# Two decoder layers on one core: 64-byte pads that shift the weight buffers and the streamed operands in SBUF

## The chip, the cores and the metric

The kernel runs on one core of one Trainium2 chip. The metric is the device time of one execution in microseconds, the median of several runs. Before the change it is 2217.02 us.

## What is computed

Two decoder layers over 256 tokens of width 2048, all in float32. The first layer mixes by sliding-window attention (32 query heads, 8 key and value heads, learned sinks), the second by a gated linear recurrence (RG-LRU). Each is followed by a gated MLP with a short causal convolution. Cut to what sets the work:

```python
D_MODEL, SEQ, DEPTH = 2048, 256, 2
QKV_DIM, D_FF = 3072, 6144

# layer 0: attention
qkv = h @ w_qkv                       # [256, 2048] @ [2048, 3072]
...
x = x + out.reshape(B, T, 2048) @ w_o
# layer 1: recurrence
xb, yb = jnp.split(h @ w_in, 2, axis=-1)   # [2048, 4096]
...
x = x + (hs * gate) @ w_out
# behind each of the two
u = causal_dwconv(h @ w_up, conv_w, conv_b)     # [2048, 12288]
g, v = jnp.split(u, 2, axis=-1)
x = x + (jax.nn.gelu(g, approximate=True) * v) @ w_down   # [6144, 2048]
```

Here `h` is the RMS-normed `x` each time.

## The kernel before

Activations stay in SBUF, transposed: features on the 128 partitions, the 256 tokens along the free axis. The weights are read once, in 373 chunks of 1 MiB (128 x 2048 float32). A chunk goes by DMA into a buffer `raw`; ScalarE casts it to `hi` (line 109), VectorE makes `lo = raw - hi` (line 117), and TensorE multiplies with both. Each of the three has three buffers in a pool of its own.

A product of two float32 numbers is taken as hi\*hi + hi\*lo + lo\*hi. A block of 128 x 128 of the weights is the stationary operand, loaded by an instruction of its own (LDWEIGHTS), and the activations are streamed past it. `mm_hi` (line 183) loads a block of `hi` and streams 512 columns, the activation's two parts side by side; `mm_lo` (line 189) loads a block of `lo` and streams 256 columns, the first part. A chunk has 16 blocks, so it costs a group of 16 matmuls of 512 columns and then a group of 16 of 256. In the MLP's down projection the chunk is taken in two halves of 8 and 8.

The products are named by their PSUM tiles: `pk`, `pq` (keys, queries), `po` (attention's output), `pu`, `pd` (MLP up and down, twice each), `px`, `py` (the recurrence's two input branches), `pr` (its output); for `pv` (values) the activation is stationary and the weight streams. The streamed operand is `h` in `pk`, `pq`, `pu`, `px` and `py`; it is `ao` in `po`, `g` in `pd` and `z` in `pr`. Between the chunks of `px` the small gate products `g<-xc` run, with `ghi` and `glo` as weights; among those of `pq` run the attention's scores `S` (lines 472 to 475, 8 matmuls for a query tile), the transposes `pT` (6) and the values `O` (line 544, 9), for 16 query tiles.

The order on every engine is written out by hand (`manual_schedule`). Where a tile lies in SBUF follows from the order of the pools and the sizes of their tiles; nothing in the code speaks of addresses:

```python
per = ctx.enter_context(tc.tile_pool(name="per", bufs=1))
rawp = ctx.enter_context(tc.tile_pool(name="rawp", bufs=3))
hip = ctx.enter_context(tc.tile_pool(name="hip", bufs=3))
lop = ctx.enter_context(tc.tile_pool(name="lop", bufs=3))
```

Of the kernel before, what the change touches and what calls it, by code (L numbers as in the profile page):

```python
"""Two decoder layers on one core: sliding-window attention with sinks + ConvFFN, then an RG-LRU
block + ConvFFN.

Activations stay on chip, transposed: features on partitions, the 256 tokens along the free
axis.  Weights stream through SBUF once, in 1 MiB chunks.  A float32 operand is split exactly into
two float32r parts (w = hi + lo, 12 significant bits each); a product is hi*hi + hi*lo + lo*hi,
accumulated in float32 in PSUM.  With the weight's part stationary, hi streams [x_hi | x_lo] and lo
streams x_hi, so a projection's PSUM bank holds hi*hi in its first half and the cross terms in its
second.

RMSNorm's per-token factor is applied to a projection's output, since it commutes with the product.
"""
# [7 lines left out]
F32 = mybir.dt.float32  # L20
# [20 lines left out]
def trunk(ctx, tc, xT, wq, wk, wv, wo, win, wg, wout, wup, wdn, mixg, ffng, kqg, sinks,  # L41
# [9 lines left out]
    rawp = ctx.enter_context(tc.tile_pool(name="rawp", bufs=3))  # L51
    hip = ctx.enter_context(tc.tile_pool(name="hip", bufs=3))
    lop = ctx.enter_context(tc.tile_pool(name="lop", bufs=3))
    ctx.enter_context(tc.manual_schedule())

    x = per.tile([P, KD, T], F32, name="x")
# [16 lines left out]

# [1 line left out]
    order = []  # L75
# [51 lines left out]
    def use():  # L127
        """The next chunk's parts."""
        c = st["use"]
        st["use"] += 1  # L130
        return his.pop(c), los.pop(c)
# [5 lines left out]
    def step(g):  # L137
        """Runs a generator to its next yield."""
        if g is not None:
            next(g, None)  # L140

# [1 line left out]
    def split_x(dst, src, gains, k):  # L143
        """dst[:, k] = the two parts of src * gain (src [P, T])."""
        act.activation(out=dst[:, k, 0, :], in_=src, func=AF.Copy, scale=gains[:, k:k + 1])
        dve.scalar_tensor_tensor(out=dst[:, k, 1, :], in0=src, scalar=gains[:, k:k + 1],
                                 in1=f(dst[:, k, 0, :]), op0=ALU.mult, op1=ALU.subtract)

    def stat(src, first):
        """sqa += src * src (src [P, 2, T])."""  # L150
        if first:
            pool.tensor_tensor(out=sqa, in0=src, in1=src, op=ALU.mult)
        else:
            pool.tensor_tensor(out=sqt, in0=src, in1=src, op=ALU.mult)  # L154
            pool.tensor_tensor(out=sqa, in0=sqa, in1=sqt, op=ALU.add)
# [5 lines left out]
    def rsqrt1(y, v):  # L161
        """A first guess of v ** -0.5."""
        act.activation(out=y, in_=v, func=AF.Ln)
        act.activation(out=y, in_=y, func=AF.Exp, scale=-0.5)

    def rsqrt2(y, v, tmp):
        """One Newton step towards v ** -0.5."""
        dve.tensor_tensor(out=tmp, in0=v, in1=y, op=ALU.mult)
        dve.scalar_tensor_tensor(out=tmp, in0=tmp, scalar=-0.5, in1=y, op0=ALU.mult, op1=ALU.mult)
        dve.scalar_tensor_tensor(out=y, in0=tmp, scalar=1.5, in1=y, op0=ALU.add, op1=ALU.mult)  # L170
# [21 lines left out]
    def x_epi(ps, d, n, gains, tp, out_=None, tag="xt"):  # L192
        """x's tiles d .. d + n take the product in ps [P, n, 512]; then h's, or the output's."""
        t = tp.tile([P, n, T], F32, tag=tag, name=f"xt{st['use']}")
# [19 lines left out]
    def late_pair(ps, rhs, mid=None):  # L214
        """Two output tiles whose operand's last two k-tiles come late."""
        parts = [use(), use()]
# [11 lines left out]
    def softplus():  # L228
        """sp = softplus(-lam) = max(-lam, 0) + log1p(e), e = exp(-|lam|), by the series of
        log1p(e) = 2 artanh(z), z = e / (2 + e) <= 1/3."""  # L230
        e, z, q = sp4, sp8, sp
# [18 lines left out]

# [1 line left out]
    def quarter(i):  # L252
# [18 lines left out]

    # ================= attention =================
    with ExitStack() as ph:
# [9 lines left out]
        ao = ap_.tile([P, KD, 2, T], F32R, name="ao")  # L283
        kq = ap_.tile([P, 1], F32, name="kq")
        kg = ap_.tile([P, 2], F32, name="kg")
        snk = ap_.tile([P, 32], F32, name="snk")
        nsnk = ap_.tile([P, 32], F32, name="nsnk")
        cb = ap_.tile([P, T], F32, name="cb")
        cc = ap_.tile([P, 2, 2], F32, name="cc")
        rc = ap_.tile([P, 2], F32, name="rc")  # L290
        rct = ap_.tile([P, 2], F32, name="rct")
        rcv = ap_.tile([P, 2], F32, name="rcv")
        bones = ap_.tile([P, P], F32, name="bones")
# [14 lines left out]
        pool.memset(maskf, 0.0)  # L308
        # key j of two blocks is seen from query i when i < j <= i + 128
        pool.affine_select(out=maskf, in_=maskf, compare_op=ALU.is_gt, fill=NEG, base=0,  # L310
# [34 lines left out]
        dve.tensor_scalar(out=kq, in0=kq, scalar1=HD ** -0.5, scalar2=None, op0=ALU.mult)  # L345
        dve.tensor_scalar(out=nsnk, in0=snk, scalar1=-1.0, scalar2=None, op0=ALU.mult)

# [1 line left out]
        ksq = {}  # L349
# [11 lines left out]
        def k_fin(p):  # L361
# [10 lines left out]
            rsqrt2(r, v, t)  # L372
            dve.scalar_tensor_tensor(out=s, in0=s, scalar=kq[:, 0:1], in1=r, op0=ALU.mult, op1=ALU.mult)
            for i in range(2):
# [4 lines left out]
        def kv_norm():  # L379
            """The first norm's factor along the free axis and along the partitions."""  # L380
            ps = psT.tile([P, 512], F32, tag="pT", name="pn")
# [33 lines left out]

# [1 line left out]
        pv = [pj.tile([P, 512], F32, tag="pj", name=f"pv{b}") for b in range(2)]  # L417
# [26 lines left out]

# [1 line left out]
        qs, pn_, pt_ = {}, {}, {}  # L446
# [31 lines left out]
        def softmax(j, S):  # L478
            # column 2 * b + a: block b, head a
            pq = S[:, 768:772]  # L480
# [13 lines left out]
            nmf = nm.rearrange("p b a -> p (b a)")  # L494
            ns = nsnk[:, 2 * j:2 * j + 2].unsqueeze(1).to_broadcast([P, 2, 2])
            dve.scalar_tensor_tensor(out=nmf, in0=mx, scalar=-1.0, in1=r, op0=ALU.mult, op1=ALU.mult)
# [38 lines left out]
        def values(j):  # L535
# [3 lines left out]
            for b in range(2):  # L539
                # (key block, slice of the transposed probabilities)  # L540
                terms = [(0, 0)] if b == 0 else [(0, 1), (1, 2)]
# [14 lines left out]
        def attend(j, ps, hi, lo, rhs, nk):  # L556
            """One output tile's products over nk of its k-tiles; between them the steps of the
            attention of the query tiles j - 1 and j - 2."""
            sm = None
# [29 lines left out]

# [1 line left out]
        head = []  # L591
# [45 lines left out]

    # ================= ConvFFN =================
    def ffn(layer, nxt):
# [62 lines left out]
    ffn(0, gm[:, 1])  # L702
    # ================= RG-LRU =================
    with ExitStack() as ph:
# [6 lines left out]
        def projected(ps, n, eng):  # L711
            """A pair of output tiles: the two halves of the bank added, times the norm's factor."""
            a = r2.tile([P, 2, T], F32, tag="a", bufs=1, name=f"pa{n}")
# [5 lines left out]

# [1 line left out]
        with ExitStack() as px:  # L721
# [48 lines left out]
            def gates_rest(n, ps):  # L770
                """r (kept in a), i * x (in u), and t = tanh(4 sp r)."""
                y = ys.pop(n)
# [48 lines left out]

# [1 line left out]
        zp = ph.enter_context(tc.tile_pool(name="z", bufs=1, reuse_waits="tile"))  # L823
        z = zp.tile([P, KD, 2, T], F32R, name="z")

        # a = exp(-8 sp r) = 1 - t (1 + a), and sqrt(1 - a a) = sqrt(t) (1 + a)
        def decay(q):
# [35 lines left out]

        # (n, i): what follows the products of tile i of the y projection's pair n, before the stream
        # moves on and after it
        before = {(2, 0): [(proj, 0)], (3, 0): [(proj, 1)], (4, 0): [(proj, 2)], (5, 0): [(proj, 3)],
# [57 lines left out]
def _layout(inp):  # L924
    import numpy as np

    def cols(w):
        """[K, N] -> [N / 128, 128, K / 128, 128]: chunk per 128 columns, rows on partitions."""
        k, n = w.shape
        return w.reshape(k // P, P, n // P, P).transpose(2, 1, 0, 3)  # L930

    def vec(v):
        """[..., n * 128] -> [128, ..., n]"""
        v = v.reshape(*v.shape[:-1], -1, P)
        return np.moveaxis(v, -1, 0)
# [47 lines left out]
```

## Time and profile before

| what | value |
|---|---|
| median of 3 runs | 2217.02 us (2216.57 to 2217.28) |
| span of the profiled execution | 2215.8 us |
| TensorE (PE) busy | 2185.9 us, 99% of the span |
| VectorE (DVE) busy | 1568.6 us, 71% |
| ScalarE (ACT) busy | 1142.7 us, 52% |
| DMA | 401.06 MB read, 51.3% of 16 engines' span |

The profiled execution's span lies 1.2 us under the median of the runs; these 1.2 us are what lies around the span. A matmul's busy time in the profile runs from its start to the end of its last column's way through the array, and the next matmul starts long before that; so how fast matmuls follow each other is read from the start times in the timeline, which joins a group of like instructions into one row, and not from the duration of one.

### The profile page before, as it was taken

Reading aid. Unit: us, or ns where it says so; the run is one execution under the profiler, and the core shown is the slowest. Engines: PE = TensorE matmul, PEld = TensorE weight load, DVE = VectorE, ACT = ScalarE, POOL = GpSimd, SP = SyncE. Lnnn points to the kernel's source line nnn. Section 1 sums busy time; section 2 is a strip of 40 time slices with the busy share of each in tenths; the row PEclk is TensorE's granted clock in tenths of the full one; section 3 lists DMA queues with packets and bytes.
Section 4 is the critical chain, followed back from the end, with each engine's and each line's share of the span. In section 5 each row is a group of like instructions: output and inputs, shape, how many; then the busy total and the mean of one; then the engine's idle time right before and its main releaser. Section 6 shows DMA issues by size and latency. Waiting matters only on the chain.

```text
span 2215.8 us, 30701 instructions
## 1 busy us (share of the span) xinstructions
PE 2185.9 (99%) x12656; PEld 1921.5 (87%) x12656; DVE 1568.6 (71%) x1862; ACT 1142.7 (52%) x1400; POOL 186.7 (8%) x155
## 2 busy tenths in 40 slices
PE   7999999999999999999999979999999999999999
PEld 6888888888888888888889868888888888888888
DVE  7877767777644777776677787777776457777654
ACT  4777445555433555553366744455554335555432
POOL 4122220000000000002200143200000000000000
PEclk9999999999999999999999999999999999999999
DMA  6333555555555555555465445555555555555543
GB/s 218 134 116 116 189 189 208 191 190 190 190 186 194 187 192 191 191 190 189 163 223 176 163 152 194 186 191 190 190 190 192 190 188 190 190 190 190 190 190 133
DMA packets 61053, 405.15 MB, mean 183 GB/s; under 512 B 7537, under 2 KB 9969, under 8 KB 13169
## 3 DMA queue, kind: packets, MB, share of 16 engines
q1 hardware_dynamic: 60912, 403.19, 51.3%
q8 instruction: 99, 1.62, 0.3%
q14 instruction: 42, 0.34, 0.0%
HBM read 401.06 MB, written 2.10 MB: 182 GB/s over the span
## 4 chain that ended last, share of the span: by engine, by line
PE 93%; DVE 3%; ACT 2%; issue 1%; POOL 1%; DMA 0%; SPq 0%; DVEq 0%; ACTq 0%
PE pu L183 32%; PE pu L189 16%; PE pd L183 16%; PE pd L189 8%; PE px L183 3%; PE po L183 3%; PE pr L183 3%; PE pq L183 2%; PE px L189 2%; PE pr L189 1%; PE po L189 1%; PE pq L189 1%; PE O L544 1%; DVE lo L117 1%; POOL ps L717 1%
## 5 line engine op out<-in xcount | busy, mean ns | idle before, releaser
L117 DVE TENSOR_TENSOR lo<-raw,hi 128x2048 fp32r<-128x2048 f32 (+1 forms) x390 | 858.1, 2200 | 223.8 <-ACT hi L109 222.6
L109 ACT CAST hi<-raw 128x2048 fp32r<-128x2048 f32 x373 | 713.0, 1912 | 386.1 <-PE pd L183 248.0
L183 PE MATMUL pu<-h,hi 128*128 128x512 f32 x3072 | 736.7, 392 | 0.0
L183 PEld LDWEIGHTS pu<-h,hi 128*128 128x128 f32 x3072 | 563.0, 188 | 111.2
L189 PEld LDWEIGHTS pu<-h,lo 128*128 128x128 f32 x3072 | 383.5, 188 | 16.4
L189 PE MATMUL pu<-h,lo 128*128 128x256 f32 x3072 | 387.0, 278 | 0.0
L183 PE MATMUL pd<-g,hi 128*128 128x512 f32 x1536 | 384.6, 392 | 0.0
L183 PEld LDWEIGHTS pd<-g,hi 128*128 128x128 f32 x1536 | 276.2, 189 | 49.4
L189 PEld LDWEIGHTS pd<-g,lo 128*128 128x128 f32 x1536 | 209.6, 190 | 14.9
L189 PE MATMUL pd<-g,lo 128*128 128x256 f32 x1536 | 214.2, 282 | 0.0
L666 ACT CAST g<-us 128x256 fp32r<-128x256 f32 x96 | 39.0, 406 | 280.7 <-DVE us L665 280.7
L659 DVE SCALAR_TENSOR_TENSOR uy<-us,fw,uy 128x255 f32<-128x255 f32 (+1 forms) x384 | 176.7, 481 | 6.8
L651 DVE TENSOR_TENSOR us<-pu,ua 128x512 f32<-128x512 f32 x96 | 66.4, 692 | 154.7 <-ACT ua L650 154.6
L650 ACT COPY ua<-pu 128x512 f32<-128x512 f32 x96 | 56.3, 587 | 143.4 <-PE pu L189 143.4
L656 ACT ACTIVATE uy<-us,fb,fw 128x256 f32<-128x256 f32 x192 | 104.8, 596 | 2.7 <-DVE us L652 2.7
L197 DVE TENSOR_TENSOR xt<-pd,x 128x512 f32<-128x512 f32 (+1 forms) x40 | 23.3, 583 | 83.3 <-PE pd L189 83.3
L154 POOL TENSOR_TENSOR sqt<-x 128x512 f32<-128x512 f32 x28 | 64.5, 2305 | 179.1 <-DVE x L198 176.6
L183 PE MATMUL px<-h,hi 128*128 128x512 f32 x320 | 77.7, 395 | 0.0
L667 DVE TENSOR_TENSOR g<-us,g 128x256 fp32r<-128x256 f32 x96 | 40.8, 425 | 45.3 <-ACT g L666 45.3
L183 PE MATMUL pr<-z,hi 128*128 128x512 f32 x256 | 63.1, 396 | 8.8 <-DVE z L861 7.8
L183 PE MATMUL pq<-h,hi 128*128 128x512 f32 x256 | 71.3, 403 | 0.2 <-DVE vh L442 0.2
L183 PEld LDWEIGHTS px<-h,hi 128*128 128x128 f32 x320 | 58.8, 189 | 11.8
(195 smaller groups left out, 1844.2 us busy)
## 6 DMA issues: line engine op xcount, KB each, us to landing
raw<-in_wup SPq DMA_DIRECT2D x192, 1024.0 KB, 4.8
raw<-in_wdn SPq DMA_DIRECT2D x96, 1024.0 KB, 4.8
raw<-in_win SPq DMA_DIRECT2D x32, 1024.0 KB, 4.8
raw<-in_wq SPq DMA_DIRECT2D x16, 1024.0 KB, 4.7
raw<-in_wo SPq DMA_DIRECT2D x16, 1024.0 KB, 4.8
raw<-in_wout SPq DMA_DIRECT2D x16, 1024.0 KB, 4.8
raw<-in_wv SPq DMA_DIRECT2D x4, 1024.0 KB, 5.4
graw<-in_wg SPq DMA_DIRECT2D x8, 512.0 KB, 3.4
```

Source lines behind the costliest of these rows:

```text
L109: act.copy(out=his[c], in_=raws[c])
L117: dve.tensor_tensor(out=los[c][:, part], in0=raws[c][:, part], in1=f(his[c][:, part]), op=ALU.subtract)
L154: pool.tensor_tensor(out=sqt, in0=src, in1=src, op=ALU.mult)
L183: pe.matmul(ps, lhsT=hi[:, off + k * n:off + k * n + P], rhs=rhs[:, xk].rearrange("p a t -> p (a t)"), start=start and k == ks[0][0], stop ...
L189: pe.matmul(ps[:, T:], lhsT=lo[:, off + k * n:off + k * n + P], rhs=rhs[:, xk, 0, :], start=False, stop=stop and k == ks[-1][0])
L197: dve.tensor_tensor(out=t[:, i], in0=ps[:, i, 0:T], in1=xs[:, i], op=ALU.add)
L650: act.copy(out=a, in_=ps[:, :, 0:T])
L651: dve.tensor_tensor(out=s, in0=ps[:, :, T:], in1=a, op=ALU.add)
L656: act.activation(out=y[:, i, :], in_=s[:, i, :], func=AF.Identity, scale=fw[:, layer, n, 2:3], bias=fb[:, layer, n:n + 1])
L659: dve.scalar_tensor_tensor(out=y[:, i, tap:], in0=s[:, i, 0:T - tap], scalar=fw[:, layer, n, 2 - tap:3 - tap], in1=y[:, i, tap:], op0=ALU. ...
L666: act.copy(out=g[:, m, 0, :], in_=s[:, 0, :])
L667: dve.tensor_tensor(out=g[:, m, 1, :], in0=s[:, 0, :], in1=f(g[:, m, 0, :]), op=ALU.subtract)
```

## The change

No instruction is added, removed or moved: on every engine the same operations stand in the same order. What changes is where tiles lie. Three pads of 64 bytes per partition are put in, one behind the last tile of `per`, one between the `hi` and the `lo` buffers, and one behind the `lo` buffers. To make room, five small tiles of the attention go: `kq` is computed in place in `kg[:, 0:1]`, `nsnk` in place in `snk`, and `rc`, `rct`, `rcv` become slices of one tile.

```diff
+    gap0 = ctx.enter_context(tc.tile_pool(name="gap0", bufs=1))
     lop = ctx.enter_context(tc.tile_pool(name="lop", bufs=3))
+    gap1 = ctx.enter_context(tc.tile_pool(name="gap1", bufs=1))
...
+    def pad(pool_, name):
+        pool_.tile([P, 16], F32, name=name)
...
+    pad(per, "pad_per")
+    pad(gap0, "pad_hl")
+    pad(gap1, "pad_lo")
...
-        kq = ap_.tile([P, 1], F32, name="kq")
         kg = ap_.tile([P, 2], F32, name="kg")
+        kq = kg[:, 0:1]
         snk = ap_.tile([P, 32], F32, name="snk")
-        nsnk = ap_.tile([P, 32], F32, name="nsnk")
...
-        rc = ap_.tile([P, 2], F32, name="rc")
-        rct = ap_.tile([P, 2], F32, name="rct")
-        rcv = ap_.tile([P, 2], F32, name="rcv")
+        rcs = ap_.tile([P, 3, 2], F32, name="rcs")
+        rc, rct, rcv = rcs[:, 0], rcs[:, 1], rcs[:, 2]
...
-        dve.tensor_scalar(out=nsnk, in0=snk, scalar1=-1.0, scalar2=None, op0=ALU.mult)
+        dve.tensor_scalar(out=snk, in0=snk, scalar1=-1.0, scalar2=None, op0=ALU.mult)
...
-            ns = nsnk[:, 2 * j:2 * j + 2].unsqueeze(1).to_broadcast([P, 2, 2])
+            ns = snk[:, 2 * j:2 * j + 2].unsqueeze(1).to_broadcast([P, 2, 2])
```

The position of a tile is its start address in a partition, modulo 128 bytes. From the tiles' sizes, which all are multiples of 32 bytes, these positions follow:

| tiles | before | after |
|---|---|---|
| `x`, `h` | 0 | 0 |
| `raw` | 64 | 0 |
| `hi` (all three) | 64 | 0 |
| `lo` (all three) | 64 | 64 |
| `ao`, `g`, `z`, `xc`, `kz`, `vh`, `ghi`, `glo`, the MLP's and the recurrence's work tiles | 64 | 0 |
| attention's `ident`, `identr`, `maskr`, `qs`, `qsq`, `qh`, `pt` | 0 | 96 |
| attention's `pr` | 64 | 32 |

All 16 blocks of a chunk, and all slices of the streamed operands, begin a multiple of 128 bytes behind their tile's start, so they have their tile's position. A weight block and the operand streamed past it stand at these positions, then:

| product | streamed, `hi`, `lo` before | streamed, `hi`, `lo` after |
|---|---|---|
| `pk`, `pq`, `pu`, `px`, `py` | 0, 64, 64 | 0, 0, 64 |
| `po`, `pd`, `pr` | 64, 64, 64 | 0, 0, 64 |

## Rows read from the trace of the kernel before

**Rows 1.** The page's head, busy times, granted clock by slice, and chain that ended last.

```profile
span 2215.8 us, 30701 instructions
PE 2185.9 (99%) x12656; PEld 1921.5 (87%) x12656; DVE 1568.6 (71%) x1862; ACT 1142.7 (52%) x1400; POOL 186.7 (8%) x155
...
PEclk9999999999999999999999999999999999999999
...
PE 93%; DVE 3%; ACT 2%; issue 1%; POOL 1%; DMA 0%; SPq 0%; DVEq 0%; ACTq 0%
```

**Rows 2.** Page, costliest groups: busy us, mean ns | idle before, its releaser.

```profile
L117 DVE TENSOR_TENSOR lo<-raw,hi 128x2048 fp32r<-128x2048 f32 (+1 forms) x390 | 858.1, 2200 | 223.8 <-ACT hi L109 222.6
L109 ACT CAST hi<-raw 128x2048 fp32r<-128x2048 f32 x373 | 713.0, 1912 | 386.1 <-PE pd L183 248.0
L183 PE MATMUL pu<-h,hi 128*128 128x512 f32 x3072 | 736.7, 392 | 0.0
...
L183 PE MATMUL pd<-g,hi 128*128 128x512 f32 x1536 | 384.6, 392 | 0.0
```

**Rows 3.** Groups of TensorE by line and shape, whole span, columns as above.

```profile
L183 PE MATMUL px<-h,hi 128*128 128x512 f32 x320 | 77.7, 395 | 0.0
L183 PE MATMUL pq<-h,hi 128*128 128x512 f32 x256 | 71.3, 403 | 0.2 <-DVE vh L442 0.2
L183 PE MATMUL pr<-z,hi 128*128 128x512 f32 x256 | 63.1, 396 | 8.8 <-DVE z L861 7.8 <-ACT hi L109 1.0
L183 PE MATMUL po<-ao,hi 128*128 128x512 f32 x256 | 62.4, 392 | 1.1 <-DVE ao L554 1.1
L183 PE MATMUL py<-h,hi 128*128 128x512 f32 x192 | 46.2, 393 | 2.8 <-ACT hi L109 1.6 <-ACT rt L839 1.3
...
L544 PE MATMUL O<-pt,vh 128*128 128x256 f32 x144 | 19.5, 280 | 0.0
```

**Rows 4.** Timeline of TensorE in an MLP's up projection: start us, us, what.

```profile
341.69 3.82 PE L183 MATMUL pu<-h,hi 128*128 128x512 f32 x16
345.35 2.05 PE L189 MATMUL pu<-h,lo 128*128 128x256 f32 x16
347.23 3.84 PE L183 MATMUL pu<-h,hi 128*128 128x512 f32 x16
350.91 1.98 PE L189 MATMUL pu<-h,lo 128*128 128x256 f32 x16
352.72 3.82 PE L183 MATMUL pu<-h,hi 128*128 128x512 f32 x16
```

**Rows 5.** Timeline of TensorE in the output projection of the attention.

```profile
296.46 3.82 PE L183 MATMUL po<-ao,hi 128*128 128x512 f32 x16
300.11 2.08 PE L189 MATMUL po<-ao,lo 128*128 128x256 f32 x16
302.02 3.82 PE L183 MATMUL po<-ao,hi 128*128 128x512 f32 x16
```

**Rows 6.** Timeline of TensorE in an MLP's down projection.

```profile
1050.62 2.00 PE L183 MATMUL pd<-g,hi 128*128 128x512 f32 x8
1052.46 1.11 PE L189 MATMUL pd<-g,lo 128*128 128x256 f32 x8
1053.42 2.00 PE L183 MATMUL pd<-g,hi 128*128 128x512 f32 x8
```

**Rows 7.** Timeline of TensorE in the recurrence's x branch.

```profile
1194.18 3.90 PE L183 MATMUL px<-h,hi 128*128 128x512 f32 x16
1197.92 2.05 PE L189 MATMUL px<-h,lo 128*128 128x256 f32 x16
1199.80 3.83 PE L183 MATMUL px<-h,hi 128*128 128x512 f32 x16
1203.47 2.05 PE L189 MATMUL px<-h,lo 128*128 128x256 f32 x16
1205.35 0.29 PE L765 MATMUL g<-xc,ghi 128*128 128x256 f32 x1
```

More of the change, by code (lines that the diff above doesn't have):

```diff
@@ L372, in k_fin @@
             rsqrt2(r, v, t)
-            dve.scalar_tensor_tensor(out=s, in0=s, scalar=kq[:, 0:1], in1=r, op0=ALU.mult, op1=ALU.mult)
+            dve.scalar_tensor_tensor(out=s, in0=s, scalar=kq, in1=r, op0=ALU.mult, op1=ALU.mult)
             for i in range(2):
```

## Prediction

> **What bounds the kernel now.** I read the page's head and its chain of waits first: the span is 2215.8 us, TensorE is busy for 2185.9 us of it, the chain that ended last is TensorE for 93%, and the granted clock is at its upper level, 2.4 GHz, in all slices [rows 1]. TensorE's idle time is small: the largest named stretches are the 8.8 us before `pr` and the 2.8 us before `py` [rows 3]. The other engines have room. VectorE's costliest group, `lo`, takes 858.1 us and waited 222.6 us for ScalarE; ScalarE's `hi` takes 713.0 us and waited 248.0 us for TensorE to free buffers [rows 2]. So the end is set by how fast one matmul follows another, and a change of SBUF positions matters if it alters that pace.
>
> The pace is in the timeline's start times. In the up projection a hi group of 16 starts at 341.69 and the lo group behind it at 345.35, so it took 3.66 us; the next took 3.68 (347.23 to 350.91). The lo groups took 1.88 (345.35 to 347.23) and then 1.81 us (350.91 to 352.72) [rows 4]. Divided by 16 these are 229 and 230 ns for 512 columns, 117.5 and 113 ns for 256. At 2.4 GHz the columns alone need 213 and 107 ns, so there is an overhead of 6 to 20 ns a matmul, and it is not constant although shape, clock and operands' positions are. In the output projection the groups take 3.65 and 1.91 us [rows 5]: hi a little faster, lo slower (119 ns). The down projection's halves take 1.84 (1050.62 to 1052.46) and 0.96 us [rows 6]; I use 0.955 for the lo half, since all starts are rounded to 0.01 and 16 matmuls at `po`'s 1.91 give twice that. What tells `pu` from `po` and `pd` is the position: `h` lies at 0 and the weights at 64, while `ao` and `g` lie at 64 like the weights.
>
> I read two things out of it. First, streamed operand and weights at the same position: hi 3.65, lo 1.91. Second, at opposite positions: hi 3.67 in the mean, lo 1.88 or 1.81. The change gives every projection the first for hi and the second for lo.
>
> **The change part by part.** A group is 16 matmuls. `pu` has 3072/16 = 192 hi groups [rows 2], `px` 20, `pq` 16, `py` 12 [rows 3], each with a lo group: 240 in all with `h`. `pd` has 1536/8 = 192 half groups [rows 2], `pr` and `po` have 16 groups each [rows 3].
>
> *Hi groups with `h`*: 3.67 to 3.65, 240 x -0.02 = -4.8 us. This carries `po`'s row over to `pu`; the 0.01 rounding of the starts makes it -2.4 to -7.2. The hi halves of `pd` and the hi groups of `po` and `pr` keep equal positions: 0.
>
> *Lo groups*: those with `h` keep opposite positions (0 and 64). `pd`, `po` and `pr` go from equal to opposite. What they get depends on which of the two paces holds, so there are two ends.
>
> At 1.81 for all: `pu` and `py` (204 groups), now 1.845 in the mean if they take turns as in [rows 4], give 204 x -0.035 = -7.1. `px` shows 1.88 twice (1197.92 to 1199.80, 1203.47 to 1205.35) [rows 7]; with `pq` taken like it, 36 x -0.07 = -2.5. `pd` goes from 0.955 to 0.905: 192 x -0.05 = -9.6. `po` and `pr`: 32 x -0.10 = -3.2. Sum -22.4.
>
> At 1.88 for all: `pu` and `py` 204 x +0.035 = +7.1; `px`, `pq` 0; `pd` 0.955 to 0.94, 192 x -0.015 = -2.9; `po`, `pr` 32 x -0.03 = -1.0. Sum +3.2.
>
> I take 1.88, for two reasons. The pace isn't a matter of positions alone, as `pu` alternates at fixed ones; it must be inherited from how the hi group before it ended. In `po` each hi group runs at the same pace and hands over alike; once all hi groups run so, the turns should end and all lo groups run at one pace. Which one? In [rows 4] the slow lo group stands behind the shorter hi group (3.66), the fast one behind the longer (3.68), and `po`'s 3.65 is next to the shorter. And in `px` [rows 7] both lo groups are slow, whether the hi group before took 3.74 or 3.67. The fast pace looks like the one that needs a special start.
>
> *The attention's small operands* move to positions 96 and 32, which nothing in the trace shows. `O` has 144 matmuls [rows 3], `S` 16 x 8 = 128, `pT` 16 x 6 = 96: 368. The paces of 256 columns seen above lie between 113 and 119 ns, so I bound each by 6 ns either way: -2.2 to +2.2 us, taken as 0, because the nearest row, `O`, had its operands at opposite positions and will have them neither equal nor opposite. `pk` and `pv` are 8 of the 373 chunks; I leave them at 0.
>
> *VectorE, ScalarE, GpSimd and DMA*: `raw` and `hi` at position 0 could change casts and subtractions. They have cover: VectorE is idle for 29% of the span, and its `lo` waits for ScalarE, which waits for TensorE [rows 1, 2]. If `hi` and `lo` both took 5% more (36 and 43 us) this would come out of that idle time; it reaches the end only where `pr` (1.0 us) and `py` (1.6 us) wait for `hi` [rows 3]. The in-place `kq` and `snk` cost the same instructions; 0.
>
> **Sum of the forecast**: 2215.8 + 1.2 around the span = 2217.0, the median of the runs; -4.8 + 3.2 = -1.6, so **2215.4 us**, and 2210 to 2221 with the bounds of the hi term and of the attention.
>
> **The rivals.** *Fast lo pace everywhere.* If the steady hi pace hands over to the 1.81 us pace, the sum is -4.8 - 22.4 = -27.2: 2189.8 us. For it speaks that `pu` holds that pace for 16 matmuls and half of its groups; against it `px`. *The lo groups go on taking turns*, in `pd` and `po` as well: mean 1.845. Then `pu` and `py` give 0, `px` and `pq` 36 x -0.035 = -1.3, `pd` 192 x -0.0325 = -6.2, `po` and `pr` 32 x -0.065 = -2.1, and hi -4.8: 2202.6 us. Against it speaks that `pu` needs two kinds of hi groups for its turns, and `po` has one.
>
> *Slower: hi groups get stuck in a third pace.* The hi group at 1194.18 took 3.74 us at the positions at which its neighbour took 3.67; it stands behind the gate products with other weights [rows 7]. After the change each hi group stands behind a lo group of the other relation of positions, as none in the trace does. If that leaves it at 3.74, it costs against my forecast 240 x 0.09 + 192 x 0.045 + 32 x 0.09 = 33 us: 2248. It becomes slower by 0.2% from 6/33, about one group in five.
>
> *The change does nothing*: the paces differ by what is streamed or by the length of the groups and not by positions. For it: `pu` and `po` differ in more than positions, and the alternation in `pu` shows a cause besides them. Time 2217. The Trainium skill ("SBUF — State Buffer", section "Who interferes with whom") would have it so: TensorE has one read port for the streamed operand and an independent one for the weights, and waits on nobody. The 1.88 against 1.91 us of lo groups of equal shape at one clock [rows 4, 5] doesn't follow from that rule, which is why it gets a small chance.
>
> **How the numbers follow.** Slow lo pace (forecast) 0.42, fast pace 0.28, turns 0.10, stuck hi 0.12, nothing 0.08. A measurement of this kernel can tell about 0.2%, 4.4 us, from no change. Faster by more than that: fast pace, turns and 0.06 of the forecast's own range, 0.44. Within: 0.33 of the forecast and nothing, 0.41. Slower: stuck hi and 0.03 of the forecast, 0.15. Cases of several signs hold the chance, so the forecast's own range is 2210 to 2221; the range that is to hold 8 in 10 goes from 2188, just below the fast pace, to 2223, and leaves out the stuck hi and the worse ends.
>
> **What would show it.** In the changed kernel's timeline: hi groups in `pu` of 3.65 us, all alike (right), or 3.74 (stuck), or 3.66 and 3.68 by turns (nothing). Lo groups in `pu` all 1.88 and in `pd` 0.94 (forecast), 1.81 and 0.905 (fast), or still 0.955 in `pd` (nothing). TensorE's share on the chain should stay above 90%; if VectorE or ScalarE gains there, the cover that I claim was not there. The hand-over from hi to lo group is the weakest step: I infer it from three groups that differ by 0.02 us.

## The result and the profile after

The changed kernel takes 2221.56 us (median of 18 runs, 2220.3 to 2222.53) against 2217.57 us before (18 runs): ratio 1.0018, 95% interval 1.0011 to 1.0024. It is slower by 4.0 us: little, but clear, since the fastest run of the changed kernel lies above the slowest of before (2218.85). The forecast was 2215.4, a little faster.

The page of the changed kernel, its head, busy times and costliest groups (busy us, mean ns | idle before, releaser), answers to [rows 1, 2]; line numbers are 11 higher:

```profile
span 2219.8 us, 30701 instructions
PE 2190.2 (99%) x12656; PEld 1925.0 (87%) x12656; DVE 1568.4 (71%) x1862; ACT 1141.6 (51%) x1400; POOL 186.2 (8%) x155
...
PE 93%; DVE 3%; ACT 1%; issue 1%; POOL 1%; DMA 0%; SPq 0%; DVEq 0%; ACTq 0%
...
L128 DVE TENSOR_TENSOR lo<-raw,hi 128x2048 fp32r<-128x2048 f32 (+1 forms) x390 | 857.9, 2200 | 224.4 <-ACT hi L120 223.1
L120 ACT CAST hi<-raw 128x2048 fp32r<-128x2048 f32 x373 | 712.8, 1911 | 387.7 <-PE pd L194 250.1
```

The span grew by 4.0 us and TensorE's busy time by 4.3; it still makes 93% of the chain. `hi` and `lo` cost ScalarE and VectorE the same as before to 0.2 us, so moving `raw` and `hi` did nothing to them. Nearly all of the change is the pace of the matmuls. The timeline of TensorE (start us, us, what) in the up projection, the output projection of the attention and the down projection, for [rows 4], [rows 5] and [rows 6]:

```profile
341.99 3.82 PE L194 MATMUL pu<-h,hi 128*128 128x512 f32 x16
345.64 2.05 PE L200 MATMUL pu<-h,lo 128*128 128x256 f32 x16
347.53 3.82 PE L194 MATMUL pu<-h,hi 128*128 128x512 f32 x16
```

```profile
296.64 3.90 PE L194 MATMUL po<-ao,hi 128*128 128x512 f32 x16
300.37 2.05 PE L200 MATMUL po<-ao,lo 128*128 128x256 f32 x16
302.26 3.90 PE L194 MATMUL po<-ao,hi 128*128 128x512 f32 x16
```

```profile
1049.94 2.02 PE L194 MATMUL pd<-g,hi 128*128 128x512 f32 x8
1051.80 1.11 PE L200 MATMUL pd<-g,lo 128*128 128x256 f32 x8
1052.75 2.02 PE L194 MATMUL pd<-g,hi 128*128 128x512 f32 x8
1054.60 1.07 PE L200 MATMUL pd<-g,lo 128*128 128x256 f32 x8
```

`pu` does what was forecast: every hi group takes 3.65 us and every lo group 1.89, and the turns have ended. In `po` the lo group came down from 1.91 to 1.89, also as forecast, but the hi group went up from 3.65 to 3.73, and in `pd` the hi halves went from 1.84 to 1.85 and 1.86. `po` and `pu` now have the same positions modulo 128 (0, 0, 64), and yet their hi groups differ by 0.08 us.

In what follows, a group's time with three decimals is the time from the start of its first matmul to the start of what follows it, the mean over all whole groups of that product in the trace. Where groups take turns at two paces, the mean lies between them.

### The profile page after: what moved, and what is told of

It reads as the page before. It is cut to its first block, busy times and chain, and to the rows that moved or that the text cites. A ratio compares the mean times of both kernels' runs of the same rounds, so it can differ in the third digit from the quotient of the medians.

```text
span 2219.8 us, 30701 instructions
## 1 busy us (share of the span) xinstructions
PE 2190.2 (99%) x12656; PEld 1925.0 (87%) x12656; DVE 1568.4 (71%) x1862; ACT 1141.6 (51%) x1400; POOL 186.2 (8%) x155
## 4 chain that ended last, share of the span: by engine, by line
PE 93%; DVE 3%; ACT 1%; issue 1%; POOL 1%; DMA 0%; SPq 0%; DVEq 0%; ACTq 0%
PE pu L194 32%; PE pu L200 16%; PE pd L194 16%; PE pd L200 8%; PE px L194 3%; PE po L194 3%; PE pr L194 3%; PE pq L194 2%; PE px L200 2%; PE pr L200 1%; PE po L200 1%; PE pq L200 1%; PE O L553 1%; DVE lo L128 1%; POOL ps L726 1%
## 5 line engine op out<-in xcount | busy, mean ns | idle before, releaser
L200 PEld LDWEIGHTS pu<-h,lo 128*128 128x128 f32 x3072 | 389.5, 189 | 14.9
L200 PE MATMUL pu<-h,lo 128*128 128x256 f32 x3072 | 394.2, 281 | 0.0
L661 DVE TENSOR_TENSOR us<-us,rb 128x512 f32<-128x512 f32 x96 | 66.5, 692 | 3.3
```

The lines of the kernel that those rows point to most:

```text
L200: pe.matmul(ps[:, T:], lhsT=lo[:, off + k * n:off + k * n + P], rhs=rhs[:, xk, 0, :], start=False, stop=stop and k == ks[-1][0])
L661: dve.tensor_tensor(out=s, in0=s, in1=rbb, op=ALU.mult)
```

## Experiments

What differs between `pu` and `po` of the changed kernel? Modulo 256, `h` starts at 128, `hi` at 128 and `lo` at 192, but `ao`, `g` and `z` at 0. So `hi` starts 0 bytes past `h` and 128 bytes past the others. **Theory 1**: the pace goes by the distances of the weights from the streamed operand modulo 256, not 128. **Theory 2**: 128 is right, and the hi groups of `po`, `pr` and `pd` are slow for what they stream or for the lo group ahead of them.

Below, a pair like (0, 64) stands for the starts of `hi` and of `lo`, in bytes past the streamed operand, modulo 256. In the kernel before the pairs are (192, 192) for `h` and (0, 0) for the others, in the changed kernel (0, 64) and (128, 192). The experiments change only where tiles lie: the 64-byte pads and small tiles of `per` (`gm` and `gf` of 128 bytes, `sp`, `sp4` and `sp8` of 64) move between four places: ahead of `h`, at the end of `per`, between `hi` and `lo`, and behind `lo`. Diffs are against the changed kernel; of tiles that only move, the new place is shown. Runs with one time are marked so.

### Only `h` moves by 128 bytes

```diff
+    gm = per.tile([P, 2, KD], F32, name="gm")
     h = per.tile([P, KD, 2, T], F32R, name="h")
...
-    gm = per.tile([P, 2, KD], F32, name="gm")
-    gf = per.tile([P, 2, KD], F32, name="gf")
...
+    gf = per.tile([P, 2, KD], F32, name="gf")
```

> Only `h` moves against the changed kernel: the tile `gm` (128 bytes) is placed ahead of it, so `h` starts 128 bytes from `hi` modulo 256, as `ao`, `g` and `z` already do; modulo 128 all positions stay. Theory 1 (the pace of a hi group goes by the distance of weights and streamed operand modulo 256): `pu`, `px`, `py` hi groups go from 3.65 to `po`'s 3.73 us, lo stay near 1.885, 224 groups x 0.08 = +18 us, about 2239 us. Theory 2 (only the position modulo 128 and what is streamed count): `pu` stays at 3.65, time of the changed kernel, about 2221 us.

Measured 2235.7 us, ratio to before 1.0082 (1.0066 to 1.0099). The up projection in the timeline:

```profile
342.54 3.90 PE L192 MATMUL pu<-h,hi 128*128 128x512 f32 x16
346.28 2.05 PE L198 MATMUL pu<-h,lo 128*128 128x256 f32 x16
348.16 3.90 PE L192 MATMUL pu<-h,hi 128*128 128x512 f32 x16
```

A hi group takes 3.74 us here (3.722 in the mean of `pu`, which has groups of 3.709 and 3.735), with every position modulo 128 as in the changed kernel. `raw`, `hi`, `lo`, `ao`, `g` and `z` lie where they lay; what moves with `h` are tiles of `per` that no projection's matmul reads. Theory 2 is out, theory 1 right to 3 us. Note that moving `h` changes both distances, from (0, 64) to (128, 192); the map below takes them apart.

### `h`, `hi` and all other streamed operands at one place modulo 256

```diff
+    gm = per.tile([P, 2, KD], F32, name="gm")
     h = per.tile([P, KD, 2, T], F32R, name="h")
...
+    p1 = gap0.tile([P, 16], F32, name="p1")
+    gf = gap1.tile([P, 2, KD], F32, name="gf")
+    p2 = gap1.tile([P, 16], F32, name="p2")
```

> Against the changed kernel `h` and `hi` are moved so that all of `h`, `ao`, `g`, `z` and `hi` start at the same place modulo 256; `lo` stays 64 bytes past. Theory 1: `po` and `pr` hi groups go back to 3.65, `pd` halves to 1.84, `pu` stays at 3.65 and 1.885: -3.2 -1.1 -0.8 = -5 us, about 2216.5 us. Theory 2 (modulo 128 only, and what is streamed): nothing moves, about 2221 us.

Measured 2216.98 us, ratio 0.9997 (0.9987 to 1.0006). This is what the prediction took the change to be: the pair is (0, 64) everywhere. The output and the down projection:

```profile
300.43 3.81 PE L192 MATMUL po<-ao,hi 128*128 128x512 f32 x16
304.08 2.05 PE L198 MATMUL po<-ao,lo 128*128 128x256 f32 x16
305.97 2.23 PE L192 MATMUL pu<-h,hi 128*128 128x512 f32 x9
```

```profile
1049.97 2.00 PE L192 MATMUL pd<-g,hi 128*128 128x512 f32 x8
1051.81 1.11 PE L198 MATMUL pd<-g,lo 128*128 128x256 f32 x8
1052.75 2.00 PE L192 MATMUL pd<-g,hi 128*128 128x512 f32 x8
```

`po`'s hi group is back at 3.65 and `pd`'s at 1.84, with a lo group at the opposite position modulo 128 still ahead of them. (`h` and `hi` lie 256 bytes apart here modulo 512, and `pu` keeps its 3.653: 256 counts as 0.)

### Without the shift of `lo`

```diff
-    p1 = gap0.tile([P, 16], F32, name="p1")
+    p1 = gap1.tile([P, 16], F32, name="p1")
```

(against the run above)

> The run with all of `h`, `ao`, `g`, `z` and `hi` at one place modulo 256, but with the pad between `hi` and `lo` taken out, so that `lo` stands at that place too. Theory (each pace goes by the distance modulo 256): `pu` lo groups at `po`'s old 1.913 us, `pd` halves at 0.953, `po` 1.913, hi at 3.654 as before: 240 x 0.027 + 192 x 0.010 + 32 x 0.027 = +9 us against the run with `lo` 64 past, about 2226 us. Rival (the lo pad has no part in it): about 2217 us.

Measured 2228.29 us (one time). The up projection:

```profile
342.70 3.82 PE L191 MATMUL pu<-h,hi 128*128 128x512 f32 x16
346.36 2.08 PE L197 MATMUL pu<-h,lo 128*128 128x256 f32 x16
348.27 3.82 PE L191 MATMUL pu<-h,hi 128*128 128x512 f32 x16
```

3.654 and 1.912: `pu` has taken the paces that `po` had before the change, and the other products have theirs of before. So what was read as two kinds of products in the trace of before was one pair of distances each. The pad between `hi` and `lo` is worth some 11 us at `hi` 0 (one time against 2216.98).

### Other pairs, two in a run

Two runs with the places of `hi` and `lo` such that `h` and the other operands see different pairs.

```diff
+    gm, sp, sp4, sp8 at the end of per
+    p1 in gap0
+    gf, p0, p2 in gap1
```

> `hi` starts 64 and `lo` 128 bytes past `h`; 192 and 0 past `ao`, `g`, `z` (modulo 256). Theory 2 (modulo 128): hi at opposite and lo at equal positions for all: `pu` hi 3.67, lo 1.91, `pd` 1.835 and 0.955, about 2232 us. Theory 1: the two groups of products differ: `h`'s lo groups, 128 apart, aren't at 1.91 like `po` of before, while `pd`'s, 0 apart, are at 0.955; hi between 3.65 and 3.74; 2215 to 2250 us.

Measured 2238.06 us (one time), paces in the table below. At (64, 128) `pu` has hi 3.722 and lo 1.898; at (192, 0) `po` has 3.661 and 1.913. Modulo 128 both are "opposite, equal", so theory 2 fails here too.

```diff
+    gm, sp ahead of h
+    sp4 at the end of per
-    gap0 = ctx.enter_context(tc.tile_pool(name="gap0", bufs=1))
+    gf, sp8, p0, p1, p2 in gap1
```

> `hi` and `lo` both start 64 bytes past `h`, and both 128 past `ao`, `g`, `z` (modulo 256). Theory 2 (modulo 128): this is the kernel before, opposite for `h` and equal for the others: `pu` 3.67 and 1.85, `po` 3.655 and 1.91, about 2217 us. Theory 1: `po`, `pr` hi at 3.73, `pd` hi halves at 1.857, together +5 us, and `pu` free to differ from 3.67 and 1.85, since 64 past is not 64 ahead: 2215 to 2235 us.

Measured 2229.18 us (one time). The up projection, at (64, 64):

```profile
343.14 3.89 PE L191 MATMUL pu<-h,hi 128*128 128x512 f32 x16
346.87 1.98 PE L197 MATMUL pu<-h,lo 128*128 128x256 f32 x16
348.68 3.89 PE L191 MATMUL pu<-h,hi 128*128 128x512 f32 x16
```

Here every lo group of `pu` takes 1.818, where at (0, 64) every one took 1.886: the same distance of `lo`, behind another hi group. So a lo group's pace depends on the hi group ahead of it too, as the prediction supposed, and the fast pace can hold throughout, but the hi group that leads to it costs 3.73.

### Looking for the fast lo pace behind a fast hi group

```diff
+    gm ahead of h
+    gf, sp, sp4 at the end of per
+    p0, p1, p2 in gap0
+    sp8 in gap1
```

> `hi` at the place of all streamed operands modulo 256, `lo` 192 bytes past instead of 64. If a lo group's pace goes by its own distance and by what the hi group before it leaves, then it runs at one pace throughout, as each hi group ends alike: either 1.885 for all, about 2217 us, or 1.813 for all, about 2192 us. If the pace went by the distance alone, the lo groups of `pu` would take turns at 1.813 and 1.885 as in the kernel before, where `lo` also stood 192 past `h`: about 2203 us. hi groups 3.654 in all three.

Measured 2232.33 us, ratio 1.0067 (1.005 to 1.0084). The up projection, at (0, 192):

```profile
342.31 3.85 PE L192 MATMUL pu<-h,hi 128*128 128x512 f32 x16
346.00 2.05 PE L198 MATMUL pu<-h,lo 128*128 128x256 f32 x16
347.88 3.85 PE L192 MATMUL pu<-h,hi 128*128 128x512 f32 x16
```

lo at one pace, 1.884, but hi at 3.689: all three expectations had 3.654. The distance of `hi` alone doesn't settle the hi pace either; the lo group beside it counts.

```diff
+    gm ahead of h
+    gf, sp at the end of per
+    p0, p1 in gap0
+    sp4, sp8, p2 in gap1
```

> `hi` 192 and `lo` 64 bytes past all streamed operands modulo 256. hi groups at 192 were seen at 3.660 to 3.675 us (`pu` before, `po` and `pr` in the run with `lo` 128 past `h`), `pd` halves at 1.848. lo groups at 64 took 1.886 behind a hi group at 0 and 1.818 behind one at 64. If what the hi group leaves decides, either is possible here: with 1.818, 240 x (-0.032) + 192 x (-0.040) + 32 x (-0.09) = -18 us, about 2199 us, with 1.886 about 2219 us.

Measured 2229.27 us, ratio 1.0053 (1.0038 to 1.0068). The up projection, at (192, 64):

```profile
343.35 3.90 PE L192 MATMUL pu<-h,hi 128*128 128x512 f32 x16
347.08 2.04 PE L198 MATMUL pu<-h,lo 128*128 128x256 f32 x16
348.96 3.90 PE L192 MATMUL pu<-h,hi 128*128 128x512 f32 x16
```

Slow in both, 3.734 and 1.884, and above either expectation. At (64, 64) a hi group of about the same length, 3.728, had 1.818 behind it, so the length of the hi group doesn't tell which lo pace follows. But the down projection's halves of 8, at the same pair, take 1.836 and 0.912, together the fastest of all runs: how a group of 16 ends up is not told by groups of 8.

```diff
-    p1 = gap0.tile([P, 16], F32, name="p1")
+    p1 = gap0.tile([P, 8], F32, name="p1")
```

(against the run with everything at one place; the 32 bytes go behind `lo`)

> As the run with all streamed operands and `hi` at one place modulo 256, but `lo` only 32 bytes past them. If steps of 64 bytes are what counts (32 belongs to 0), lo groups take 1.913 as at distance 0: about 2226 us. If 32 belongs to 64, they take 1.886: about 2217 us. If finer steps count, the lo pace is a third one, 1.82 to 1.95 us: 2195 to 2235 us.

Measured 2228.22 us (one time). The up projection, at (0, 32):

```profile
341.94 3.84 PE L192 MATMUL pu<-h,hi 128*128 128x512 f32 x16
345.62 2.05 PE L198 MATMUL pu<-h,lo 128*128 128x256 f32 x16
347.51 3.84 PE L192 MATMUL pu<-h,hi 128*128 128x512 f32 x16
```

3.682 and 1.892, neither those at 0 nor those at 64: finer steps than 64 bytes count.

### A version that beats both

The best pair for groups of 16 is still that of `pu` before, (192, 192), with 3.669 + 1.850 = 5.519 us. So the next run gives it to all products.

```diff
-    gap0 = ctx.enter_context(tc.tile_pool(name="gap0", bufs=1))
+    gm = per.tile([P, 2, KD], F32, name="gm")
     h = per.tile([P, KD, 2, T], F32R, name="h")
...
+    gf = per.tile([P, 2, KD], F32, name="gf")
+    sp = per.tile([P, KD], F32, name="sp")
+    sp4 = gap1.tile([P, KD], F32, name="sp4")
+    sp8 = gap1.tile([P, KD], F32, name="sp8")
+    p0 = gap1.tile([P, 16], F32, name="p0")
+    p1 = gap1.tile([P, 16], F32, name="p1")
+    p2 = gap1.tile([P, 16], F32, name="p2")
```

> `hi` and `lo` both 192 bytes past all streamed operands modulo 256: for `h` the distances of the kernel before, at other absolute positions; for `ao`, `g`, `z` new. Theory (the two distances modulo 256 settle the pace of both groups): `pu` as before, hi 3.659 and 3.677 and lo 1.813 and 1.885 by turns, `po` and `pr` the same pattern instead of 3.654 and 1.913, 32 x -0.048 = -1.5 us; `pd` halves free between the best and the worst seen at 192 (1.836 to 1.848 and 0.91 to 0.943), 192 x -0.005 to -0.046 = -1 to -9 us: 2207 to 2216 us. Rival (absolute positions count too): `pu` shows other paces, 2215 to 2240 us.

Measured **2208.48 us**, ratio to before 0.9955 (0.9938 to 0.9971). The output and the down projection:

```profile
294.53 2.05 PE L197 MATMUL po<-ao,lo 128*128 128x256 f32 x16
296.42 3.84 PE L191 MATMUL po<-ao,hi 128*128 128x512 f32 x16
300.09 1.98 PE L197 MATMUL po<-ao,lo 128*128 128x256 f32 x16
301.91 3.82 PE L191 MATMUL po<-ao,hi 128*128 128x512 f32 x16
305.57 2.04 PE L197 MATMUL po<-ao,lo 128*128 128x256 f32 x16
```

```profile
1050.27 2.00 PE L191 MATMUL pd<-g,hi 128*128 128x512 f32 x8
1052.10 1.07 PE L197 MATMUL pd<-g,lo 128*128 128x256 f32 x8
1053.01 1.99 PE L191 MATMUL pd<-g,hi 128*128 128x512 f32 x8
1054.83 1.11 PE L197 MATMUL pd<-g,lo 128*128 128x256 f32 x8
```

`po` now shows the turns of [rows 4], 3.66 and 3.67 for hi, 1.89 and 1.82 for lo, and `pu` is as it was before at other absolute positions. `pd` gains 192 x (1.841 + 0.953 - 1.831 - 0.926) = 7.1 us, `po` and `pr` some 1.5.

### The rest of the map

```diff
+    gm, sp ahead of h
+    gf, sp4, sp8 at the end of per
+    p0, p1 in gap0
+    p2 in gap1
```

> `hi` at `h`'s place and `lo` 128 bytes past it; 64 and 192 past `ao`, `g`, `z`. The hi pace was 3.654 behind lo groups at 0 and 64, 3.682 behind 32, and 3.689 behind 192. If the lo group decides how the hi group behind it starts, `pu` hi is between 3.65 and 3.70 and lo between 1.81 and 1.92; `po` hi, 64 from its operand, at 3.72 to 3.73 as in the two runs at 64: 2200 to 2240 us. If a hi group's pace went by its own distance alone, `pu` hi is 3.654 and `po` 3.725.

Measured 2231.4 us (one time). The up projection, at (0, 128):

```profile
342.65 3.81 PE L192 MATMUL pu<-h,hi 128*128 128x512 f32 x16
346.30 2.08 PE L198 MATMUL pu<-h,lo 128*128 128x256 f32 x16
348.22 3.81 PE L192 MATMUL pu<-h,hi 128*128 128x512 f32 x16
```

The fastest hi groups of all, 3.643, with the slowest lo groups, 1.924, just outside the 1.92 expected.

```diff
+    gm, sp ahead of h
+    sp4 at the end of per
+    p0, p1, p2 in gap0
+    gf, sp8 in gap1
```

> `hi` 64 bytes past `h` and `lo` at its place; 128 and 64 past `ao`, `g`, `z`. If own distance decides the hi pace, `pu` hi is at 3.72 to 3.73 as in the two runs at 64 and `po` at 3.72 to 3.735 as in those at 128: 2230 to 2245 us. If the lo group before decides as much, one of them leaves these values by over 0.02 us: 2195 to 2245 us. lo groups at 0 took 1.913 to 1.918 in all runs so far, behind hi at 0 and at 192; behind hi at 64 the same by distance alone.

Measured 2239.27 us (one time): `pu` 3.738 and 1.895 at (64, 0), `po` 3.715 and 1.855 at (128, 64). hi by own distance held within 0.01; lo at distance 0 did not stay at 1.913. The output projection, at (128, 64), where lo takes turns:

```profile
295.20 1.98 PE L198 MATMUL po<-ao,lo 128*128 128x256 f32 x16
297.02 3.87 PE L192 MATMUL po<-ao,hi 128*128 128x512 f32 x16
300.73 2.05 PE L198 MATMUL po<-ao,lo 128*128 128x256 f32 x16
302.62 3.65 PE L192 MATMUL po<-ao,hi 128*128 128x512 f32 x15
```

```diff
+    sp4 ahead of h
+    gf, sp and 32 bytes at the end of per
-    gap0 = ctx.enter_context(tc.tile_pool(name="gap0", bufs=1))
+    gm, sp8, p1, p2 and 32 bytes in gap1
```

> `hi` and `lo` both 224 bytes past `h`, and both 160 past `ao`, `g`, `z` (modulo 256), each 32 bytes beside the 192 of the best run. If the start counts in steps of 64, `h`'s and the others' groups run like those at 192 (3.668 and 1.850, `pd` 1.831 and 0.926, about 2208 us) or like those at 0 and 128 (3.654 and 1.913; 3.722 and 1.898, `pd` 1.862 and 0.948: about 2230 us). If 32 bytes make a pace of their own, as `lo` 32 past did (hi 3.682 and lo 1.892, neither 0's nor 64's), then `pu` is away from all of these by over 0.01 us in one group: 2195 to 2245 us.

Measured 2242.53 us (one time), the slowest. The up projection, at (224, 224):

```profile
343.18 3.89 PE L191 MATMUL pu<-h,hi 128*128 128x512 f32 x16
346.92 2.03 PE L197 MATMUL pu<-h,lo 128*128 128x256 f32 x16
348.78 3.89 PE L191 MATMUL pu<-h,hi 128*128 128x512 f32 x16
```

32 bytes beside the best pair costs 0.06 us for a hi group.

All pairs, in us; the fourth column is the 8 hi and the 8 lo matmuls of a `pd` half, where the pair occurred there:

| pair | hi of 16 | lo of 16 | `pd` hi, lo | seen in |
|---|---|---|---|---|
| (0, 0) | 3.654 | 1.913 | 1.841, 0.953 | before (`po`), without shift of `lo` |
| (0, 32) | 3.682 | 1.892 | 1.843, 0.947 | `lo` 32 past |
| (0, 64) | 3.654 | 1.886 | 1.837, 0.943 | changed kernel (`pu`), all at one place |
| (0, 128) | 3.643 | 1.924 | | `lo` 128 past (`pu`) |
| (0, 192) | 3.689 | 1.884 | 1.870, 0.943 | `lo` 192 past |
| (64, 0) | 3.738 | 1.895 | | `hi` 64 past, `lo` at 0 (`pu`) |
| (64, 64) | 3.728 | 1.818 | | both 64 past (`pu`) |
| (64, 128) | 3.722 | 1.898 | | `hi` 64, `lo` 128 past (`pu`) |
| (64, 192) | 3.722 | 1.884 | 1.861, 0.943 | `lo` 128 past (`po`) |
| (128, 64) | 3.715 | 1.855 | 1.857, 0.923 | `hi` 64 past, `lo` at 0 (`po`) |
| (128, 128) | 3.723 | 1.899 | 1.862, 0.948 | both 64 past (`po`) |
| (128, 192) | 3.733 | 1.885 | 1.857, 0.934 | changed kernel (`po`) |
| (160, 160) | 3.734 | 1.922 | 1.867, 0.959 | both 224 past (`po`) |
| (192, 0) | 3.661 | 1.913 | 1.848, 0.938 | `hi` 64, `lo` 128 past (`po`) |
| (192, 64) | 3.734 | 1.884 | 1.836, 0.912 | `hi` 192, `lo` 64 past |
| (192, 192) | 3.669 | 1.850 | 1.831, 0.926 | before (`pu`), best version |
| (224, 224) | 3.733 | 1.867 | | both 224 past (`pu`) |

hi is fast at `hi` 0 and at most of 192 (3.643 to 3.689), slow at 64, 128, 160 and 224 (3.715 to 3.738). The pair doesn't settle everything: in the changed kernel `pr` is at 3.709 where `po` is at 3.733, in the run that moved `h` the hi groups of `pu` went from 3.735 to 3.709 at one pair, and before the change `px` had hi groups of 3.67 and of 3.74 [rows 7] at `pu`'s pair. What else enters (how the group begins, after a pause or after other products) is not separated here. And `raw` starts at the same place modulo 256 as `hi` in every run, so the map can't tell the two apart; but the work on `raw` doesn't set the paces. In the changed kernel the last weights land at 2195.5 us, the last cast ends at 2199.7 and the last subtraction at 2202.6, and the four hi halves of `pd` that start after that take 1.855 to 1.860 us, like those before.

## Why the prediction was wrong

*The bound* was right: TensorE alone, no cover lost, ScalarE and VectorE unchanged.

*Hi groups with `h`*, forecast -4.8: `pu` 192 x (3.654 - 3.669) = -2.9, `px` 20 x (3.651 - 3.696) = -0.9, `py` -0.2, and `pq`, whose groups the attention interrupts, -0.4 in all; together -4.4. Right.

*Lo groups*: for `h` the choice of the slow pace was right: `pu` 192 x (1.886 - 1.850) = +6.9, `py` +0.2, `px` +0.1 (forecast +7.1). Half of its ground held: once the hi groups were alike, the turns ended. The other half did not: at (64, 64) steady hi groups of 3.728 have the fast pace, 1.818, behind them throughout, and at (192, 64) hi groups of 3.734 have 1.884. So that the slow pace came out, and not the fast one, was partly luck. `pd` 192 x (0.934 - 0.953) = -3.6 (forecast -2.9) and `po` and `pr` 32 x -0.028 = -0.9 (-1.0) were luck as well, for they stand at (128, 192) and not at (0, 64): the lo halves of `pd` follow at 0.91, 0.94 and 0.95 us by turns, and at (0, 64) they take 0.943, which would be -1.9. `pq` gave -0.6 (0). Sum +2.1 against +3.2.

*The step that failed* is "The hi halves of `pd` and the hi groups of `po` and `pr` keep equal positions: 0." They keep them modulo 128 and lose them modulo 256: `hi` goes from 0 to 128 past `ao`, `g` and `z`, and `lo` from 0 to 192 instead of 64. It cost `pd` 192 x (1.857 - 1.841) = +3.1, `po` 16 x (3.733 - 3.655) = +1.2 and `pr` 16 x (3.709 - 3.654) = +0.9: +5.2 us where 0 stood. The sum becomes -4.4 + 2.1 + 5.2 = +2.9; the span grew by 4.0. Of the last 1.1 us, 0.4 is `pr`'s longer wait (8.8 to 9.2 us), 0.4 `pk` and 0.3 `O` and `S`, all three taken as 0. The run with everything at one place modulo 256 is the forecast with that step made true: 2216.98 us, 0.8 under the 2217.75 of before beside it, where 1.6 less was forecast; its interval holds both that and no change.

Which of the two distances costs it? For a group of 16 the table has all four cases: 3.654 at (0, 64), 3.715 with `hi` alone at 128, 3.689 with `lo` alone at 192, 3.733 with both. There `hi`'s own distance is the larger part. For the halves of `pd` the same cases are 1.837, 1.857, 1.870 and 1.857: there either distance costs as much as both, or more. So the forecast's account, in which a hi group goes by its own operands' positions, fails in this too.

The 1.2 us "around the span" set one run's span against the median of others; in the runs that have both it is about 1.8 us (2221.57 and 2219.8 in the changed kernel). It stands on both sides and moves nothing.

The trace of before couldn't show the step wrong: it has only the pairs (192, 192) and (0, 0), which a rule modulo 128 and one modulo 256 tell apart equally well. What the prediction could have seen is that it had two pairs and drew a rule from them: that `hi` moves to 128 past `g` was in the code's sizes, and "no row shows it" would have given the term a range up to the 3.74 of [rows 7], as the attention's operands had one.

*The rivals.* "Stuck hi" had the pace right (3.73 in `po`) and the mechanism at most in part: it named the opposite lo group ahead of a hi group as the cause. With that left in place, at (0, 64), `po` returns to 3.65; at (0, 192) it stays at 3.69, so which lo group stands ahead does count. "Does nothing" is out: moving one streamed tile by 128 bytes moves the time by 14 us. The Trainium skill ("SBUF — State Buffer", section "Who interferes with whom") gives TensorE two independent read ports and names no cost of placement. The runs here, from 2208 to 2243 us with the same instructions in the same order, show such a cost.

## What to carry to other kernels

Where TensorE is the bound and its matmuls follow each other without a wait, compare start-to-start times of equal matmuls in different stages; if they differ, look at where weights and streamed operand start in SBUF; in this kernel it was modulo 256 bytes that counted, not 128. A rule from two placements is not a rule: give an unseen distance a range as wide as the paces seen, and try placements in one run each, two per run where two operands can be put at different distances. Placement is also fragile: a 64-byte tile put between a streamed operand and the weights' buffers changes their distance, and with it, here, the pace of every matmul on them.

## What the runs showed that was not expected

- The same matmul of 512 columns follows its predecessor after 227.7 to 233.6 ns in the mean (3.643 and 3.738 us for 16), one of 256 columns after 113.6 to 120.3 (1.818 and 1.924), by placement alone, at a granted clock of 0.994 to 0.996.
- The fastest hi and the fastest lo groups don't come together: (0, 128) has 3.643 with 1.924, (64, 64) has 1.818 with 3.728. The sum is smallest at (192, 192), where lo takes turns at 1.81 and 1.88.
- Groups of 8 and of 16 rank the pairs differently: (192, 64) has the best `pd` halves (2.748 us) and one of the worst sums in `pu` (5.618).
- What in the chip makes these paces is not shown by any run here.
